# A decoder block on one core: the place at which the second half's normalised input is computed

## The chip, the cores and the metric

The kernel runs on one core of a Trainium2 chip. The metric is device time in microseconds (us), taken as the median over several runs. A profile is one further execution that the hardware profiler recorded; its own time is given beside its span.

## The reference

One layer of a decoder block for a sequence of 1024 tokens of width 1024. What matters here is the first part: a normalised and modulated input `h`, a wide projection of it, two branches with gates, and their merge.

```python
mod = silu(c) @ w_ada + b_ada
shift1, scale1, gate1, shift2, scale2, gate2 = split(mod, 6)
h = modulate(rms_norm(x, norm1_w), shift1, scale1)      # h * (1 + scale) + shift
q, k, v, r, a_lr, su, sv, g_a, g_b = split(h @ w_in)
...
o_gla = rms_norm(gla_chunked(q, k, v, log_a), gla_norm_w) * silu(r)
o_sgu = spatial_gating(gelu(su), gelu(sv), sgu_w, sgu_b, sgu_ln_w, sgu_ln_b)
merged = sigmoid(g_a) * o_gla + sigmoid(g_b) * o_sgu
x = x + gate1 * (merged @ w_out)
h2 = modulate(rms_norm(x, norm2_w), shift2, scale2)
x = x + gate2 * peer(h2, ...)                           # product-key experts, top 16 of 16384
return rms_norm(x, final_norm_w)
```

`h` of a token depends on `x` and `c` alone. So `h` of the later tokens can be computed at any time before their projection.

## The kernel before

The sequence is worked off in two halves of 512 tokens (`hf` = 0 and 1). A half goes through the weight groups in this order: G_V0, G_V1, G_QK0, G_QK1 (with the linear attention's heads between them), G_SV0, G_SV1, G_R0, G_R1, G_A0, G_A1, G_SU0, G_SU1, G_B0, G_B1, then the output projection, the second norm and the routing of the experts. The second half also carries the experts' work of the first.

A weight group is a matrix of 1024 x 512. `group` calls `stream`, which runs over eight slices `k` of 128 rows. A slice is loaded on SP's queue into `wt` (five buffers, line 1386), split into a high part `wh` by ScalarE (ACT, line 1390) and a low part `wl` by VectorE (DVE, line 1392), four buffers each, and multiplied by TensorE (PE) with the high and low parts of `h`, which lie in `hTh` and `hTl`: three products for each of four PSUM banks `mm`, so 12 matmuls a slice (lines 184 to 187, and 190 to 192 for the first and the last slice) and 96 a group. Weights are made up to three slices ahead. After the last slice the four banks are evicted by the group's own function:

- `ev_r` (G_R0, G_R1): ACT computes tanh into `sg`, DVE multiplies with the bank (line 1624) and then with `ot` (line 1626). The bank is free after DVE's first operation.
- `ev_a` (G_A0, G_A1): ACT computes tanh (line 1632), DVE multiplies `ot` (line 1634). The bank is free after ACT.
- `ev_su` (G_SU0, G_SU1): ACT computes gelu into `us` (line 1449). The bank is free after ACT.
- `ev_b` (G_B0, G_B1): ACT computes tanh, DVE takes two operations on `us` and `ot`. The bank is free after ACT.

After each of G_SU0 and G_SU1 comes `mix(c)`: 16 matmuls of 128 x 128 into the same four banks (`sps`, line 1651) and 16 DVE operations that take them out (line 1655).

Side work is written as Python generators in queues. Each slice of `stream` ends with `step()`, which pumps each queue: one `next` for `qa` and one for `qm`. In the first half `qa` holds, from the end of the first group on, four `ada_row` generators (each sums eight slices of `w_ada` and stores a row of the modulation, 11 pumps) and, behind them, `next_h(HALF)` (14 pumps). `qm` holds the norms of the branches, `out_norm` and `gate_norm`; it is emptied by `qm.drain()` ahead of each `mix`. `qa.drain()` stands at the end of a half.

`next_h` computes `h` for the second half and stores it in `hn_d` in device memory. Four pumps load two tiles `xb` each (SP, line 1198) and square them on ACT with a running sum (line 1199). One pump makes the row of reciprocal roots: a sum and a multiply on DVE, a power on POOL, `dg` on DVE, a product of `ones` and `dg` on PE (line 1188), a copy `rrow` on ACT (line 1189). Nine pumps run over eight tiles: load `xt` (SP, line 1209), scale it (DVE, line 1212), round to `hi` with the shift (ACT, line 1215), take the rest `lo` (DVE, line 1216), and store both to `hn_d` (ACT's queue, line 1218). A load of slice k is emitted one pump ahead of its use. `xb` and `xt` share two buffers, `hi` has two and `lo` one. Each load on SP is held behind the weight load that was made last before it (`tc.issue_after(last_wt[0])`).

The second half begins by loading `hn_d` into `hTh` and `hTl` (line 1402).

The program is written in this order, and the build then lays out each engine's instruction order from simulated times (`schedule_with_timeline_sim=True`); `issue_after` pins an instruction behind another on its engine. On the chip every engine runs its list in order, and waits for semaphores.

Of the kernel before, what the change touches and what calls it, by code (L numbers as in the profile page):

```python
# [21 lines left out]
HALF = 512  # L22
# [59 lines left out]
def block_kernel(ctx: ExitStack, tc: tile.TileContext, x, xT, cT, w_ada, b_ada, b_adaT, n1T, w_inp, w_alr,  # L82
# [95 lines left out]
    def mm3s(sets, k):  # L178
        if k in (0, KD - 1):
            for ps, lh, ll, rh, rl, feat in sets:  # L180
                mm3(ps, lh, ll, rh, rl, k == 0, k == KD - 1)
            return
        for ps, lh, ll, rh, rl, feat in sets:
            nc.tensor.matmul(ps, lh, rh, start=False, stop=False)  # L184
            nc.tensor.matmul(ps, *((lh, rl) if feat else (ll, rh)), start=False, stop=False)  # L185
        for ps, lh, ll, rh, rl, feat in sets:
            nc.tensor.matmul(ps, *((ll, rh) if feat else (lh, rl)), start=False, stop=False)  # L187
# [857 lines left out]
    qa, qr, qp, qdir, qm, qf = Queue(), Queue(), Queue(), Queue(), Queue(), Queue()  # L1045
# [10 lines left out]
    with ExitStack() as pa:  # L1056
# [105 lines left out]
        def ada_row(c, r):  # L1162
            for acc in ada_acc(c):
                yield
            for _ in range(2):
                yield
            row_ = t4("adarow")
            nc.scalar.dma_start(row_[0:1], b_ada[:, c * D:(c + 1) * D])
            for n in range(2):
                sl = slice(n * 512, (n + 1) * 512)  # L1170
                ps = auxt([1, 512])
                nc.tensor.matmul(ps, ones[:, 0:1], acc[:, sl], start=True, stop=True)
                nc.vector.tensor_tensor(row_[0:1, sl], row_[0:1, sl], ps, op=OP.add)
            if r == 1:
                nrow = t4("nrow")
                nc.scalar.dma_start(nrow[0:1], n2_w)
                nc.vector.scalar_tensor_tensor(row_[0:1], row_[0:1], 1.0, nrow[0:1], op0=OP.add, op1=OP.mult)
            nc.scalar.dma_start(rows_d[r:r + 1, :], row_[0:1])
            yield

        def rstd_row(ss, eng, rrow):
            rstd = sm_p.tile([P, BH], F32, name="rstd")
            rstd_of(rstd, ss, D, eng)
            dg = t2("dg")
            nc.vector.tensor_tensor(dg.rearrange("p (i q) -> p i q", q=P), ident.unsqueeze(1).to_broadcast([P, BH, P]),
                                    rstd.unsqueeze(2).to_broadcast([P, BH, P]), op=OP.mult)
            rps = auxt([P, HALF])
            nc.tensor.matmul(rps, ones, dg, start=True, stop=True)
            nc.scalar.activation(rrow, rps, AF.Identity)
            return rrow  # L1190

        def next_h(t0):
            ss = sm_p.tile([P, 2, BH], F32, name="ss")
            for i in range(BH):
                for n in range(2):
                    xb = gl.tile([P, HALF], F32, name="xb", tag="qs")
                    with tc.issue_after(last_wt[0]):
                        nc.sync.dma_start(xb, x[t0 + i * P:t0 + (i + 1) * P, n * HALF:(n + 1) * HALF])
                    nc.scalar.activation(xb, xb, AF.Square, accum_out=ss[:, n, i:i + 1])
                yield  # L1200
            nc.vector.tensor_tensor(ss[:, 0], ss[:, 0], ss[:, 1], op=OP.add)
            rrow = rstd_row(ss[:, 0], nc.vector, gl.tile([P, HALF], F32, name="rrow", tag="ktok", bufs=1))
            yield
            xts = []
            for k in range(KD + 1):
                if k < KD:
                    xts.append(gl.tile([P, HALF], F32, name="xt", tag="qs"))
                    with tc.issue_after(last_wt[0]):
                        nc.sync.dma_start(xts[k], xT[k * P:(k + 1) * P, t0:t0 + HALF])
                if k:  # L1210
                    j, xt = k - 1, xts[k - 1]
                    nc.vector.scalar_tensor_tensor(xt, xt, scol[:, j:j + 1], rrow, op0=OP.mult, op1=OP.mult)
                    hi = gl.tile([P, HALF], F32R, name="hi", tag="kk")
                    lo = gl.tile([P, HALF], F32R, name="lo", tag="kt", bufs=1)
                    nc.scalar.activation(hi, xt, AF.Identity, bias=mod[:, j:j + 1])
                    nc.vector.scalar_tensor_tensor(lo, xt, mod[:, j:j + 1], hi.bitcast(F32), op0=OP.add, op1=OP.subtract)
                    for n, t in enumerate((hi, lo)):
                        nc.scalar.dma_start(hn_d[:, n, j], t.bitcast(F32))
                yield
# [176 lines left out]
        for hf in range(NHALF):  # L1396
# [7 lines left out]
            def stream(srcs, body, evac, npsum=4, post=None, again=False):  # L1404
                pss = [mm.tile([P, 512], F32, name="mm", tag="mm") for _ in range(npsum)]
                turn = WS // len(srcs) if again else 0
                for n in range(KD):
                    weights_ahead(LOOK + 1)
                    ws = [made.pop(0) for _ in srcs]
                    body((n - turn) % KD, ws, pss, n)  # L1410
                    if post and n in post:
                        post[n]()
                    step()
                for i in range(npsum):
                    evac(i, pss[i])

            def group(src, evac, feat, post=None):
                def body(k, ws, pss, n):
                    wh, wl = ws[0]
                    cuts = [slice(i * P, (i + 1) * P) for i in range(4)]  # L1420
                    if feat:
                        mm3s([(pss[i], wh[:, cs], wl[:, cs], hTh[:, k], hTl[:, k], True) for i, cs in enumerate(cuts)], n)
                    else:
                        mm3s([(pss[i], hTh[:, k, cs], hTl[:, k, cs], wh, wl, False) for i, cs in enumerate(cuts)], n)

                stream([src], body, evac, post=post)
# [18 lines left out]
            def ev_su(c):  # L1445
                def f(i, ps):
                    if c == 0:
                        us[i] = t4("us")
                    nc.scalar.activation(us[i][:, c * 512:(c + 1) * 512], ps, AF.Gelu)
                return f  # L1450
# [18 lines left out]
            if hf == 0:  # L1469
                with tc.issue_after(hlast[0]):  # L1470
                    nc.scalar.dma_start(wst, wsT)
                for g in range(8):
                    nc.gpsimd.affine_select(out=wst[:, g], in_=wst[:, g], pattern=[[1, P]], compare_op=OP.is_ge, fill=0.0,
                                            base=0, channel_multiplier=-1)
                for c, r in ((2, 0), (4, 1), (3, 2), (5, 3)):
                    qa.add(ada_row(c, r))
                qa.add(next_h(HALF))

            alh = t2("alh", F32R)
            all_ = t2("all_", F32R)  # L1480
# [139 lines left out]
            def ev_r(c):  # L1620
                def f(i, ps):
                    sg = t2("sg")
                    nc.scalar.activation(sg, ps, AF.Tanh, scale=0.5)
                    nc.vector.scalar_tensor_tensor(sg, sg, 1.0, ps, op0=OP.add, op1=OP.mult)  # L1624
                    o = ot[i][:, c * 512:(c + 1) * 512]
                    nc.vector.tensor_tensor(o, o, sg, op=OP.mult)
                return f

            def ev_a(c):
                def f(i, ps):  # L1630
                    sg = t2("sg")
                    nc.scalar.activation(sg, ps, AF.Tanh, scale=0.5)
                    o = ot[i][:, c * 512:(c + 1) * 512]
                    nc.vector.scalar_tensor_tensor(o, sg, 1.0, o, op0=OP.add, op1=OP.mult)
                return f
# [44 lines left out]
            qm.add(gate_norm())  # L1680
            for gid, ev in ((G_R0, ev_r(0)), (G_R1, ev_r(1)), (G_A0, ev_a(0)), (G_A1, ev_a(1))):
                group(w_inp[gid], ev, False)
            for c in range(2):
                group(w_inp[G_SU0 + c], ev_su(c), False)
                qm.drain()
                mix(c)
# [228 lines left out]
```

## Time and profile before

| | |
|---|---|
| median of 3 runs | 1419.35 us (1417.38 to 1422.0) |
| profiled execution | 1417.0 us, span 1415.3 us |
| mean granted TensorE clock | 0.976 of full speed |
| PE busy | 1346.5 us, 95% of the span |
| DVE busy | 1076.7 us, 76% |
| ACT busy | 698.2 us, 49% |
| POOL busy | 274.3 us, 19% |
| DMA | 348.15 MB, mean 246 GB/s |

Times in the profile are us from the span's start. A row of a timeline has the start, the length, the engine, the line of the kernel, the operation, what it writes and reads, and in brackets how long the engine had been idle before it and what ended that. A row of a stretch has, for each engine, the busy time and the number of instructions, then the granted clock, the DMA engines' share and GB/s. A row of a source line has the least, middle and greatest duration in ns, and the first and last start.

In the first half G_R1 ends at 259.4, G_A0 at 284.5, G_A1 at 306.3, G_SU0 at 328.0 and G_SU1 at 353.4; the instructions of `next_h` lie between 213 and 288.

### The profile page before, as it was taken

To read this page: it belongs to the slowest core of one execution; us is meant where nothing else is said; L and a number is where in the kernel's file an instruction comes from. 1 tells how busy PE (TensorE), PEld (TensorE's weight loads), DVE (VectorE), ACT (ScalarE), POOL (GpSimd) and SP (SyncE) were. 2 spreads that over 40 slices of the span, in tenths; PEclk is the share of its full clock that TensorE was granted. 3 is DMA by queue.
4 is the path that set the end of the run, shared out by engine and by line. 5 is a ranking of instruction groups with operands and counts; after the bars stand their busy time and mean duration, and the time that the engine had idled before them with its cause. 6 is when DMAs were issued, how large, how long until landed. Compare 5 with 4: busy or idle time off the path is not lost.

```text
span 1415.3 us, 19579 instructions
## 1 busy us (share of the span) xinstructions
PE 1346.5 (95%) x5998; PEld 1037.7 (73%) x5998; DVE 1076.7 (76%) x3066; ACT 698.2 (49%) x1568; POOL 274.3 (19%) x271
## 2 busy tenths in 40 slices
PE   8999999999999899998999999999998999889996
PEld 6678777788888888777777788887777876444553
DVE  7785778543458578798879788878798877799885
ACT  4454335333245355474444566555555554555552
POOL 0000002000000021332452142211111123444421
PEclk9999999999999999999999999999999999989999
DMA  9753556642257469857787699986688568897984
GB/s 325 240 210 125 179 161 214 221 133 88 84 168 243 156 203 325 280 146 267 245 295 263 226 345 342 328 327 227 219 313 296 196 228 313 340 362 302 416 299 190
DMA packets 123492, 348.15 MB, mean 246 GB/s; under 512 B 15385, under 2 KB 24857, under 8 KB 111346
## 3 DMA queue, kind: packets, MB, share of 16 engines
q0 software_dynamic: 31488, 163.85, 31.5%
q1 hardware_dynamic: 72240, 133.44, 28.1%
q10 hardware_dynamic: 19650, 49.54, 9.7%
q8 instruction: 48, 0.79, 0.2%
q14 instruction: 66, 0.54, 0.1%
HBM read 318.35 MB, written 28.42 MB: 245 GB/s over the span
## 4 chain that ended last, share of the span: by engine, by line
PE 43%; DVE 8%; DMA 6%; ACT 4%; issue 3%; POOL 0%; ACTq 0%; DVEq 0%; POOLq 0%
PE mm L184 7%; PE mm L185 7%; PE mm L187 6%; PE acc L609 6%; PE mm L190 3%; PE mm L191 2%; PE mm L192 2%; PE aux L1805 2%; DMA uv<-in_tab_dram,dix 2%; DVE uv L583 1%; PE hps L581 1%; DMA uvd<-in_down_dram,dix 1%; PE hps L582 1%; PE acc L628 1%; PE acc L629 1%
## 5 line engine op out<-in xcount | busy, mean ns | idle before, releaser
L1390 ACT ACTIVATE wh<-wt 128x512 fp32r<-128x512 f32 x344 | 212.4, 628 | 269.2 <-PE mm L185 117.3
L1392 DVE TENSOR_TENSOR wl<-wt,wh 128x512 fp32r<-128x512 f32 x344 | 231.4, 684 | 116.8 <-ACT wh L1390 54.9
L184 PE MATMUL mm<-wh,hTh 128*128 128x512 f32 x648 | 256.8, 397 | 3.5 <-ACT wh L1390 3.5
L185 PE MATMUL mm<-wh,hTl 128*128 128x512 f32 x648 | 256.0, 395 | 0.0
L187 PE MATMUL mm<-wl,hTh 128*128 128x512 f32 x648 | 203.1, 397 | 0.7 <-DVE wl L1392 0.7
L184 PEld LDWEIGHTS mm<-wh,hTh 128*128 128x128 f32 x648 | 122.5, 189 | 32.6 <-ACT wh L1390 4.3
L185 PEld LDWEIGHTS mm<-wh,hTl 128*128 128x128 f32 x648 | 122.4, 189 | 26.3 <-issue 0.8
L187 PEld LDWEIGHTS mm<-wl,hTh 128*128 128x128 f32 x648 | 121.0, 189 | 27.3 <-issue 1.3
L528 POOL DMA_INDIRECT uv<-in_tab_dram,ix x74 | 77.0, 1041 | 263.9 <-ACT ix L560 137.2
L184 PE MATMUL mm<-hTh,wh 128*128 128x512 f32 x240 | 96.8, 403 | 0.1
L185 PE MATMUL mm<-hTl,wh 128*128 128x512 f32 x240 | 95.0, 396 | 0.0
L583 DVE SCALAR_TENSOR_TENSOR uv<-uv,hps 128x512 f32<-128x512 f32 x112 | 74.6, 680 | 21.7 <-DMA uv<-in_tab_dram,ix 12.9
L190 PE MATMUL mm<-wh,hTh 128*128 128x512 f32 x216 | 86.4, 408 | 2.7 <-DVE sg L1624 2.7
L192 PE MATMUL mm<-wh,hTl 128*128 128x512 f32 x216 | 85.5, 396 | 0.0
L191 PE MATMUL mm<-wl,hTh 128*128 128x512 f32 x216 | 85.3, 395 | 0.1
L190 PE MATMUL mm<-hTh,wh 128*128 128x256 f32 (+1 forms) x208 | 71.5, 346 | 6.0 <-DVE q L1528 5.0
L191 PE MATMUL mm<-hTl,wh 128*128 128x256 f32 (+1 forms) x208 | 70.1, 338 | 3.8 <-DVE hTl L176 3.8
L187 PE MATMUL mm<-hTh,wl 128*128 128x512 f32 x240 | 71.7, 397 | 0.7 <-DVE wl L1392 0.7
L192 PE MATMUL mm<-hTh,wl 128*128 128x256 f32 (+1 forms) x208 | 68.7, 337 | 0.0
L621 DVE SCALAR_TENSOR_TENSOR vl<-uv,r,vh 128x512 fp32r<-128x512 f32 x82 | 59.7, 745 | 9.5 <-ACT vh L620 4.1
L609 PE MATMUL acc<-uv,W 128*128 128x512 f32 x132 | 63.3, 602 | 1.4 <-ACT W L598 0.8
L755 POOL DMA_INDIRECT uvd<-in_down_dram,dix x32 | 33.7, 1054 | 157.1 <-DVE dix L1790 40.0
(957 smaller groups left out, 2889.1 us busy)
## 6 DMA issues: line engine op xcount, KB each, us to landing
wt<-in_w_inp_dram SPq DMA_DIRECT2D x224, 256.0 KB
wt<-in_w_qp_dram SPq DMA_DIRECT2D x72, 256.0 KB
wada<-in_w_ada_dram SPq DMA_DIRECT2D x32, 512.0 KB
wt<-in_w_outp_dram SPq DMA_DIRECT2D x56, 256.0 KB
wada<-in_w_ada_dram SPq DMA_DIRECT2D x32, 256.0 KB
s_d<-so ACTq DMA_DIRECT2D x28, 256.0 KB
xt<-in_xT_dram SPq DMA_DIRECT2D x16, 256.0 KB
xr<-in_x_dram ACTq DMA_DIRECT2D x8, 512.0 KB
```

The lines of the kernel that those rows point to most:

```text
L184: nc.tensor.matmul(ps, lh, rh, start=False, stop=False)
L185: nc.tensor.matmul(ps, *((lh, rl) if feat else (ll, rh)), start=False, stop=False)
L187: nc.tensor.matmul(ps, *((ll, rh) if feat else (lh, rl)), start=False, stop=False)
L190: nc.tensor.matmul(ps, lh, rh, start=first, stop=False)
L191: nc.tensor.matmul(ps, lh, rl, start=False, stop=False)
L192: return nc.tensor.matmul(ps, ll, rh, start=False, stop=last).ins
L528: nc.gpsimd.indirect_dma_start(out=dst[:], out_offset=None, in_=src, in_offset=off)
L583: nc.vector.scalar_tensor_tensor(uv[0][:, sl], uv[0][:, sl], 1.0, hps, op0=OP.mult, op1=OP.mult, accum_out=r[:, 2 + n:3 + n])
L609: ins = nc.tensor.matmul(acc[:, sl], W, v[:, sl], start=first, stop=last).ins
L621: nc.vector.scalar_tensor_tensor(vl, v, r[:, 5:6], vh.bitcast(F32), op0=OP.mult, op1=OP.subtract)
L1390: nc.scalar.activation(wh, wt, AF.Identity)
L1392: nc.vector.tensor_tensor(wl, wt, wh.bitcast(F32), op=OP.subtract)
```

## The change

The line that adds `next_h(HALF)` to the queue `qa` is taken from behind the four `ada_row` and put behind the group G_A1 of the first half, ahead of G_SU0. By then `qa` is empty. Everything that `next_h` issues is the same; only the steps in which it is pumped differ.

```diff
                 for c, r in ((2, 0), (4, 1), (3, 2), (5, 3)):
                     qa.add(ada_row(c, r))
-                qa.add(next_h(HALF))
...
             qm.add(gate_norm())
             for gid, ev in ((G_R0, ev_r(0)), (G_R1, ev_r(1)), (G_A0, ev_a(0)), (G_A1, ev_a(1))):
                 group(w_inp[gid], ev, False)
+            if hf == 0:
+                qa.add(next_h(HALF))
             for c in range(2):
                 group(w_inp[G_SU0 + c], ev_su(c), False)
                 qm.drain()
```

## The prediction, made before the changed kernel was run

> **What bounds the kernel now.** I read the page's first two parts, then the busy time by stretch, one stretch for each weight group around the change, then TensorE's timeline for gaps, and last the rows of the moved work and what waited for it.
>
> ```profile
> span 1415.3 us, 19579 instructions
> PE 1346.5 (95%) x5998; PEld 1037.7 (73%) x5998; DVE 1076.7 (76%) x3066; ACT 698.2 (49%) x1568; POOL 274.3 (19%) x271
> core 0: us, PE busy (x) PEld busy (x) DVE busy (x) ACT busy (x) POOL busy (x), PEclk, DMA share, GB/s
> 213.00:243.00 30.00, 30.00 (x127) 22.94 (x126) 26.16 (x43) 15.17 (x35) 7.22 (x5) 1.00 0.69 234
> 243.00:281.00 38.00, 35.54 (x154) 28.46 (x153) 22.36 (x34) 15.07 (x25) 0.00 (x0) 1.00 0.61 205
> 281.00:305.00 24.00, 24.00 (x107) 19.79 (x107) 11.37 (x18) 9.24 (x16) 0.00 (x0) 1.00 0.49 159
> 305.00:328.00 23.00, 23.00 (x103) 19.05 (x102) 8.17 (x12) 8.41 (x15) 0.00 (x0) 1.00 0.31 95
> ```
>
> TensorE (PE) is busy 95% of the span, and in the first half's merge stage nearly without a break: only the stretch 243:281 has idle time (35.54 of 38 us). So what a move of DVE, ACT and DMA work can win or lose here is the gaps that it takes from PE or gives to it. The timeline of PE shows them:
>
> ```profile
> 259.36 0.39 PE L192 MATMUL mm<-wh,hTl 128*128 128x512 f32 x1
> 260.59 0.50 PE L190 MATMUL mm<-wh,hTh 128*128 128x512 f32 x1 [0.85 <-DVE sg L1624]
> 262.54 0.39 PE L187 MATMUL mm<-wl,hTh 128*128 128x512 f32 x1
> 263.85 0.50 PE L190 MATMUL mm<-wh,hTh 128*128 128x512 f32 x1 [0.93 <-DVE sg L1624]
> 274.41 0.39 PE L185 MATMUL mm<-wh,hTl 128*128 128x512 f32 x1
> 275.49 1.20 PE L187 MATMUL mm<-wl,hTh 128*128 128x512 f32 x4 [0.69 <-DVE wl L1392]
> ...
> 284.46 0.39 PE L192 MATMUL mm<-wh,hTl 128*128 128x512 f32 x1
> 306.25 0.39 PE L192 MATMUL mm<-wh,hTl 128*128 128x512 f32 x1
> 328.01 0.39 PE L192 MATMUL mm<-wh,hTl 128*128 128x512 f32 x1
> 811.37 0.50 PE L190 MATMUL mm<-wh,hTh 128*128 128x512 f32 x1 [0.91 <-DVE sg L1624]
> ```
>
> The rows at 259.36, 284.46, 306.25 and 328.01 are the last matmuls of the groups G_R1, G_A0, G_A1 and G_SU0. Their distances are 25.10, 21.79 and 21.76 us. A group is 96 matmuls, so one is 0.227 us and a step (12 matmuls) 2.72 us, and G_A0 is 3.33 us too long. The three gaps account for it. Taken start to start, less one matmul, they are 260.59 - 259.36 - 0.23 = 1.00, 263.85 - 262.54 - 0.23 = 1.08 and 275.49 - 274.41 - 0.23 = 0.85, together 2.93. The other 0.4 is the slower first matmul behind each gap (0.50 against 0.39), so I count 0.13 more for each: 1.13, 1.21 and 0.98.
>
> **The change, part by part.** Nothing is added or removed; the generator next_h moves in the queue qa. Before, it stood behind four ada_row of 11 pumps each, so with one pump a step its first pump was the 45th after the first group: step 4 of G_R0. Now it is added behind G_A1 and its first pump is step 0 of G_SU0: 3 + 8 + 8 + 8 + 1 = 28 steps later, 28 x 2.72 = 76 us. Its 14 pumps then end at step 5 of G_SU1. What moves:
>
> ```profile
> L1198 SPq DMA_DIRECT2D xb<-in_x_dram x8: 327/354/532, 213.3 to 228.0; - x8
> L1199 ACT ACTIVATE xb<-xb x8: 615/632/632, 217.3 to 231.0; 128x512 f32<-128x512 f32 x8
> L1209 SPq DMA_DIRECT2D xt<-in_xT_dram x8: 328/328/681, 230.4 to 276.1; - x8
> L1212 DVE SCALAR_TENSOR_TENSOR xt<-xt,scol,rrow x8: 744/752/753, 243.6 to 280.4; 128x512 f32<-128x512 f32 x8
> L1215 ACT ACTIVATE hi<-xt,mod x8: 722/724/730, 244.4 to 281.2; 128x512 fp32r<-128x512 f32 x8
> L1216 DVE SCALAR_TENSOR_TENSOR lo<-xt,mod,hi x8: 745/748/752, 245.1 to 286.4; 128x512 fp32r<-128x512 f32 x8
> L1218 ACTq DMA_DIRECT2D hn_d<-lo x8: 326/361/362, 246.8 to 287.2; - x8
> ```
>
> That is 16 loads on SP, 16 stores on ACT's queue (eight hi beside the eight lo), 8 x 0.63 + 8 x 0.72 = 10.8 us of ACT, 8 x 0.75 + 8 x 0.75 = 12 us of DVE, a few small operations, one power on POOL and one product of ones and dg on PE. The product costs PE the same in either place: nothing. The power no longer stands behind gate_norm's on POOL (five in 213:243, none from 243 on): nothing, since rrow is not waited for by PE.
>
> The consumer of hn_d is the second half's first load:
>
> ```profile
> L1402 SPq DMA_DIRECT2D hTl<-hn_d x8: 319/356/819, 541.1 to 561.2; - x8
> ...
> 264.32 0.75 DVE L1216 SCALAR_TENSOR_TENSOR lo<-xt,mod,hi 128x512 fp32r<-128x512 f32 x1
> 265.09 0.33 SPq L1209 DMA_DIRECT2D xt<-in_xT_dram  x1
> 269.16 0.75 DVE L1212 SCALAR_TENSOR_TENSOR xt<-xt,scol,rrow 128x512 f32<-128x512 f32 x1 [0.49 <-DMA xt<-in_xT_dram]
> 269.95 0.73 ACT L1215 ACTIVATE hi<-xt,mod 128x512 fp32r<-128x512 f32 x1 [5.99 <-DVE xt L1212]
> 274.08 0.75 DVE L1212 SCALAR_TENSOR_TENSOR xt<-xt,scol,rrow 128x512 f32<-128x512 f32 x1 [3.51 <-DMA xt<-in_xT_dram]
> ```
>
> The last store was issued at 287.2 and will be near 287 + 76 + 3.5 = 367 (3.5 for the mix between the groups): still 170 us ahead of the load at 541. Costed at nothing; that cover would have to shrink by 170 us.
>
> What does cost is these waits. Two xt buffers make a chain: a load of xt goes out when lo has released the buffer (lo ends 265.07, load 265.09), lands some 4 us later, and then xt, hi, lo follow. DVE works in order and sat up to 3.51 us before an xt; ACT sat 5.99 us before a hi, and SP held the weight loads behind the xt load. That made G_A0's second gap (DVE was at an xt when G_R1's eviction sg had to be made) and the third (wl late behind the 3.51 us wait). Those two go: 1.21 + 0.98 = 2.2 us. The first gap (1.13) I leave: at the same boundary of the second half, where no next_h runs, the row at 811.37 shows the same wait of 0.91. So the removal is worth 2.2, between 2.2 and 3.3.
>
> The same chain now runs from about 320 (243.6 + 76) to 367, through G_SU0's end, mix(0), G_SU1, mix(1) and into G_B0. There the end of a group looks like this:
>
> ```profile
> 326.40 2.64 ACT L1449 ACTIVATE us<-mm 128x512 f32<-128x512 f32 x4 [0.95 <-PE mm L192]
> 328.24 3.73 PE L1651 MATMUL sps<-svg,wst 128*128 128x128 f32 x32
> 329.41 1.12 DVE L1655 SCALAR_TENSOR_TENSOR us<-sps,sgub,us 128x128 f32<-128x128 f32 x4 [2.94 <-PE sps L1651]
> 331.73 0.48 PE L190 MATMUL mm<-wh,hTh 128*128 128x512 f32 x1
> ```
>
> The first of the four gelu evictions ends about 326.40 + 0.66 = 327.1, and PE needs its bank at 328.24: 1.2 us to spare on ACT. The first us eviction ends at 330.5 and PE needs the bank at 331.73: 1.2 us on DVE. At mix(0) the first two xt are due, which were loaded long before; the waits begin with the third. At mix(1), near 353.6, the seventh and eighth are due (76 + 3.5 after their old times, the last at 280.4 + 79.5 = 360). So one boundary, on two engines, is exposed. Bounds: nothing, or ACT's 5.99 less 1.2, 4.8 us, and DVE's 3.5 less 1.2, 2.3 us, 7.1 together. I take 1.2, what the like collision cost at 263.85, the nearest row, and half of the 0.98 of a late wl: 38 us of this chain brought one such, and beside next_h DVE is loaded about as before ((22.36 - 12) in 38 us there, 8.17 in 23 here), so I give it an even chance. Together 1.7.
>
> Sum: -2.2 + 1.7 = -0.5 us on the profiled execution, which took 1417.0 us (1.7 around its span); that lies 2.35 under the median of the three runs, 1419.35. I put the difference on the median: 1418.9. Less than 0.3% (4.3 us) can hardly be told from no change here.
>
> A rule weighed: the xt waited for at 269.16 had been issued at 265.09, 4.1 us before, at 205 GB/s, and the first xb needed 4.0 (213.3 to 217.3) at 234, so I take the waits over unchanged; the new stretch has 95 and what next_h brings. [...]
>
> **Rivals.**
> (a) Slower: one stall at mix(1) that is long enough to lower PE's clock. What such a stall costs is seen later in this trace:
>
> ```profile
> 470.60 0.58 PE L191 MATMUL mm<-hTl,wh 128*128 128x256 f32 x1 [2.57 <-DVE hTl L176]
> 465.00:470.00 5.00, 2.07 (x17) 1.62 (x15) 4.96 (x27) 2.56 (x6) 0.00 (x0) 0.98 0.56 213
> 470.00:475.00 5.00, 4.40 (x20) 4.40 (x21) 1.84 (x3) 0.63 (x1) 0.00 (x0) 0.50 0.02 3
> 475.00:480.00 5.00, 5.00 (x38) 5.00 (x37) 1.79 (x3) 1.89 (x3) 0.00 (x0) 0.83 0.32 107
> ```
>
> PE was idle 2.9 us of 465:470, and the granted clock was 0.50 in the next five and 0.83 in the five after: 2.5 + 0.85 = 3.35 us lost beyond the stall. The price here: ACT's 4.8 + 3.35 - 2.2 = +6.0, 1425.3. It decides from a gelu held back by more than 1.2 + 2.9 = 4.1 us. For it: ACT has sat 5.99 us behind one xt. Against: that was one wait in eight. [...]
> (b) Faster: the waits miss mix(1), and the shifted order also removes the pit at 465 to 480 (3.35): -3.3 - 3.35 = -6.7, 1412.7. The build lays out each engine's order from simulated times, so later orders can shift. For it: only that; nothing links the pit with next_h, which is through 100 us before.
> (c) The change doesn't do what it says: the layout starts next_h as early as its inputs allow, and its old place comes back. For: its first load went out some 15 us ahead of its step (213.3, while step 4 of G_R0 ends near 228: G_R1's end at 259.36 less a group, the product and three steps). Against: each load is held behind the last weight load made before it, so 76 us can't be gained. It gives 1419.35.
>
> **How the numbers follow.** The forecast with (c), and all sizes between -4.3 and +4.3: 0.62 (forecast 0.57, c 0.05). (a), or the same through later orders that get worse: 0.21. (b): 0.17. The forecast's own range is 1415.1 to 1423.6. The range for 8 in 10 reaches to most of both others: 1413.5 to 1425.5.
>
> **What would show it.** In the changed profile the xt rows lie between about 318 and 362, G_A0 is about 22 to 23 us long (from the last matmul of G_R1 to its own), the gaps of 0.93 and 0.69 are gone, and PE has new gaps near mix(1) or G_B0's start, released by gelu, us or wl, of 1 to 3 us. Wrong would be: a gap at G_B0 or G_SU1 above 4 us with a clock under 1.00 behind it; no new gap at all; or a time that differs by more than 4 us with this stretch alike, so that the difference came from behind 380 us, where I expect every stretch alike.

## The result: slower by about half a per cent

The changed kernel took 1424.02 us in the median of 20 runs, the kernel before on the same chip 1417.46 in the median of 20. The ratio is 1.0053, 95% interval 1.0035 to 1.0071. The forecast's likeliest case was no change; what came is nearest to rival (a): stalls with a lowered clock behind one of them, but at the ends of three groups and not at one.

The profiled execution of the changed kernel took 1415.62 us, the shortest of its 20 runs, so spans can't be compared as they stand: TensorE had a lead of 4.67 us before the moved work begins, over the same instructions in the same order (G_R0's first matmul starts at 208.41 instead of 213.08). I therefore compare a stage of TensorE's work: from the products of line 1172, inside G_R0, to the first product of line 1806 (before: 1805), behind G_B1 and the output projection. Before, the first loads and squares of the moved work lie up to 11 us ahead of this mark, but they cost TensorE nothing there: at the products the lead is still 4.67 us (219.38 instead of 224.05). First the kernel before, its two marks and the stage in one row (us, busy time of PE, PEld, DVE, ACT, POOL with instructions, granted clock, DMA share, GB/s):

```profile
224.05 1.45 PE L1172 MATMUL aux<-adacc,ones 128*1 128x512 f32 x3
462.76 1.94 PE L1805 MATMUL aux<-keyst,qt 128*128 128x128 f32 x15 [0.21 <-ACT qt L1772]
224.05:462.76 238.71, 235.34 (x1127) 195.01 (x1126) 138.62 (x234) 94.41 (x163) 7.36 (x7) 1.00 0.50 164
```

The changed kernel's page, and the same stage with the stretches around the move:

```profile
span 1413.9 us, 19574 instructions
PE 1337.7 (95%) x5998; PEld 1029.8 (73%) x5998; DVE 1077.3 (76%) x3066; ACT 697.6 (49%) x1568; POOL 277.6 (20%) x271
219.38:463.91 244.53, 236.88 (x1127) 196.17 (x1126) 138.42 (x233) 96.21 (x171) 7.37 (x7) 0.99 0.50 165
243.00:281.00 38.00, 38.00 (x170) 31.45 (x169) 16.34 (x25) 12.06 (x21) 0.00 (x0) 1.00 0.34 110
281.00:305.00 24.00, 21.73 (x96) 17.60 (x95) 8.37 (x15) 12.23 (x28) 1.01 (x1) 1.00 0.51 165
328.30:333.30 5.00, 4.95 (x15) 3.93 (x16) 5.00 (x15) 0.72 (x1) 0.00 (x0) 0.66 0.61 212
333.30:338.30 5.00, 5.00 (x24) 4.14 (x23) 1.43 (x3) 0.65 (x1) 0.00 (x0) 1.00 0.47 154
```

The same 1127 matmuls take 244.53 us instead of 238.71, 5.8 more. The old place is clean now: in 243 to 281 PE is busy for 38.00 of 38 us, where it was busy for 35.54. The loss has moved behind 281. TensorE's timeline shows where:

```profile
297.30 0.39 PE L192 MATMUL mm<-wh,hTl 128*128 128x512 f32 x1
299.95 0.50 PE L190 MATMUL mm<-wh,hTh 128*128 128x512 f32 x1 [2.27 <-ACT sg L1631]
...
325.81 0.72 PE L1650 MATMUL sps<-svg,wst 128*128 128x128 f32 x5
328.35 0.50 PE L190 MATMUL mm<-wh,hTh 128*128 128x512 f32 x1 [1.81 <-DVE us L1654]
...
329.72 0.63 PE L185 MATMUL mm<-wh,hTl 128*128 128x512 f32 x1
330.15 0.63 PE L187 MATMUL mm<-wl,hTh 128*128 128x512 f32 x1
...
351.61 0.39 PE L192 MATMUL mm<-wh,hTl 128*128 128x512 f32 x1
354.67 3.81 PE L1650 MATMUL sps<-svg,wst 128*128 128x128 f32 x32 [2.67 <-ACT us L1449]
```

There are three stalls, one at each end of a group that the moved work now passes, where there were three smaller ones in G_A0:

- Start of G_SU0: 299.95 - 297.30 - 0.23 = 2.42, with the slower first matmul (0.13) 2.55 us. PE waits for ACT's tanh out of the bank.
- Start of G_SU1, behind mix(0): idle 1.81; as these rows overlap by 0.24 where nothing waits (before: 328.24 + 3.73 against 331.73), and with the 0.13, 2.2 us. PE waits for DVE's eviction of the mix. Behind it the clock is 0.66 for five us: matmuls are 0.43 apart (329.72, 330.15) instead of 0.23. That is 5 x 0.34 = 1.7 us more.
- mix(1): 354.67 - 351.61 - 0.23 = 2.83 us. PE waits for ACT's gelu.

Together 9.3 us. Against the 3.3 us by which G_A0 was too long, that makes +6.0; the stage has +5.8. What the engines were doing at these three places is in their timelines. ACT:

```profile
290.00 0.63 ACT L1199 ACTIVATE xb<-xb 128x512 f32<-128x512 f32 x1 [3.44 <-DMA xb<-in_x_dram]
...
298.69 0.63 ACT L1199 ACTIVATE xb<-xb 128x512 f32<-128x512 f32 x1 [0.46 <-DMA xb<-in_x_dram]
299.32 0.58 ACT L1631 ACTIVATE sg<-mm 128x512 f32<-128x512 f32 x1
...
353.55 0.33 ACTq L1218 DMA_DIRECT2D hn_d<-lo  x1
353.93 2.06 ACT L1449 ACTIVATE us<-mm 128x512 f32<-128x512 f32 x4 [3.11 <-DVE lo L1216]
```

The tanh at 299.32 could have run when the bank was done, before 298; it stands in ACT's list behind a square of `xb` that waited for its load until 298.69. The gelu at 353.93 stands behind the issue of `lo`'s store at 353.55, which waits for `lo`. And DVE:

```profile
325.84 0.75 DVE L1212 SCALAR_TENSOR_TENSOR xt<-xt,scol,rrow 128x512 f32<-128x512 f32 x1 [3.02 <-DMA xt<-in_xT_dram]
326.51 0.74 DVE L1216 SCALAR_TENSOR_TENSOR lo<-xt,mod,hi 128x512 fp32r<-128x512 f32 x1
327.17 1.12 DVE L1654 SCALAR_TENSOR_TENSOR us<-sps,sgub,us 128x128 f32<-128x128 f32 x4
...
352.77 0.75 DVE L1216 SCALAR_TENSOR_TENSOR lo<-xt,mod,hi 128x512 fp32r<-128x512 f32 x1 [3.04 <-DMA hn_d<-lo]
```

The eviction of the mix at 327.17 stands behind an `xt` that sat 3.02 us for its load, and its `lo`. The `lo` at 352.77 waited 3.04 us until the store of the `lo` before it had read the one buffer. So the stall at mix(1) is a chain: store of `lo` to device memory, `lo` on DVE, store on ACT's queue, gelu on ACT, mix on PE.

### The profile page after: what moved, and what is told of

Its sections match the earlier page's. It is cut to its first block, busy times and chain, and to the rows that moved or that the text cites. A ratio compares the mean times of both kernels' runs of the same rounds, so it can differ in the third digit from the quotient of the medians.

```text
span 1413.9 us, 19574 instructions
## 1 busy us (share of the span) xinstructions
PE 1337.7 (95%) x5998; PEld 1029.8 (73%) x5998; DVE 1077.3 (76%) x3066; ACT 697.6 (49%) x1568; POOL 277.6 (20%) x271
## 4 chain that ended last, share of the span: by engine, by line
PE 39%; DVE 10%; DMA 7%; issue 4%; ACT 4%; POOL 0%; another core or an unknown queue 0%; DVEq 0%; ACTq 0%; POOLq 0%
PE mm L184 6%; PE mm L185 6%; PE mm L187 6%; PE acc L609 5%; PE mm L190 2%; PE mm L191 2%; PE mm L192 2%; DMA uvd<-in_down_dram,dix 2%; DMA uv<-in_tab_dram,ix 2%; DVE uv L583 2%; PE aux L1806 2%; DMA uv<-in_tab_dram,dix 1%; PE hps L581 1%; PE hps L582 1%; DVE uv L537 1%
```

## The experiments

The theories, by the names that the expectations use. **Q**, the in-order theory: ACT and DVE work their lists in order, and an instruction of `next_h` that waits (for a landing, or for a buffer that a store still reads) holds up the eviction behind it, so the cost arises only at ends of groups. **E**: the loss lies elsewhere, in a later stage. **M**: the loads land later in the new place. **D**: the place itself decides; the later `next_h` comes, the slower. E needs no experiment of its own: outside the stretch from 213 to 354 us, from G_R0 to mix(1), each engine has the same order of instructions before and after, but for four places behind 900 us where neighbours on ACT or DVE are swapped; on POOL the order is the same throughout. Medians and ratios are against the kernel before, run on the same chip; "stage" is the time between the two marks, 238.7 before and 244.5 after. (The stretch of 170.9 us in the expectations of e0 to e3 is a part of it.)

**Again, both kernels.** e0 and e10 are the changed kernel unaltered, e8 and e9 the kernel before; the last three are single executions.

> The changed kernel once more, for a second profile. Theory Q (in-order queues blocked by next_h at the ends of groups): the three gaps of TensorE come back at the same places, at the start of G_SU0 behind sg, at the start of G_SU1 behind us, at mix(1) behind gelu, 1.5 to 3 us each, and the stretch from the first matmuls of G_R0 to those of G_B1 takes 175 to 179 us, against 170.9 in the profile of before. The whole is 0.3% to 0.7% slower than before. Theory E (elsewhere: the loss does not lie in this stretch, since the profiled execution of the changed kernel was not longer than that of before): the gaps change place or go, and the stretch is within 2 us of 171. Theory M (memory: the loads land later in the new place): loads of xt need clearly more than the 3.5 to 4.4 us of before.

> The kernel before, for a second profile. Open is why the kernels with five buffers, whose time from adacc to keyst is 236.8 and 236.9 us against 238.7 in the one profile of before, are not 0.15% faster than before. Theory Q: the gaps of before in G_A0 (1.0, 1.1 and 0.85 us start to start) differ between executions, and here they sum to less: the time from adacc to keyst lies at 236.5 to 238. Rival: the gaps are the same in each execution (238.5 to 239), and the five buffers cost 2 to 3 us somewhere else.

> The kernel before, for a third profile. As for the second: Theory Q 236.5 to 238 us from adacc to keyst, with gaps that differ from the other two profiles; rival 238.5 to 239.

> The changed kernel, for a third profile. Theory Q: gaps at the starts of G_SU0, G_SU1 and mix(1) again, 1 to 4 us each, with 244 to 248 us from adacc to keyst; and the times of the three executions differ by how long the waits were and whether the granted clock fell behind one.

Measured: e0 1424.49 against 1413.91, ratio 1.0074 [1.0045, 1.0102], stage 247.32, with stalls at the same three places; e10 1422.5, stage 247.71. The kernel before took 1414.45 and 1412.76 (and 1405.83 in a further execution beside them, so that single executions tell little), stage 238.47 and 238.64, each time with its three gaps in G_A0 (0.64, 1.02, 0.58 and 0.71, 0.45, 1.18 us of idle time). I had expected 236.5 to 238; the loss in G_A0 is there each time, and its sum hardly varies. The three stages of the changed kernel (244.5, 247.3, 247.7) lie 7.9 us above the three of before (238.7, 238.5, 238.6) in the mean, 0.56% of 1417, against 0.53% and 0.74% between the medians: the whole difference lies in the stage. In e10 rival (a) stands in plain view at mix(1): PE, its stretches, and DVE's wait for `lo`'s store:

```profile
359.59 5.25 PE L1650 MATMUL sps<-svg,wst 128*128 128x128 f32 x32 [4.97 <-ACT us L1449]
354.60:359.60 5.00, 0.03 (x2) 0.04 (x1) 1.35 (x2) 1.38 (x3) 0.00 (x0) 0.96 0.44 143
359.60:364.60 5.00, 5.00 (x33) 5.00 (x33) 2.85 (x10) 1.83 (x4) 0.00 (x0) 0.70 0.28 87
357.70 0.75 DVE L1216 SCALAR_TENSOR_TENSOR lo<-xt,mod,hi 128x512 fp32r<-128x512 f32 x1 [3.99 <-DMA hn_d<-lo]
```

PE stood still for 4.97 us, and the mix behind it took 5.25 us instead of 3.81, at a clock of 0.70.

**More buffers, at the changed place.** e1 gives the loads of `xb` and `xt` five buffers instead of two and issues those of `xb` one pump and those of `xt` two pumps earlier; e2 takes `lo` from a pool of five buffers that it shares with other tiles (`t2`), instead of from its single one; e3 does both. (Where the expectations of e11 and e12 give `lo` two buffers, it is this pool too.)

```diff
 # e1
+tag, bufs = (("qs", 2), ("qs", 2), ("adc", 3), ("adc", 3), ("adc", 3))[nring[0] % 5]
+t = gl.tile([P, HALF], F32, name=name, tag=tag, bufs=bufs)
...
-if k < KD:   # load xt[k]
+if k + 2 < KD:   # load xt[k + 2]
 # e2
-lo = gl.tile([P, HALF], F32R, name="lo", tag="kt", bufs=1)
+lo = t2("lo", F32R)
```

> Changed place, and the loads of xb and xt go through five buffers instead of two and are issued two pumps earlier; orders behind the stretch are the same as in the changed kernel. Theory Q: the gaps at G_SU0 (sg behind the squares) and G_SU1 (us behind an xt) go, the one at mix(1) stays, since lo still has one buffer: the stretch takes 169.5 to 172.5 us, the whole 0.1% to 0.4% faster than the changed kernel, within 0.2% of before. Theory E: no change, 0.5% slower than before. Theory M: loads land as late or later with more of them in flight, the waits of DVE before xt stay at 14 us in sum, and the time stays.

> Changed place, and lo is written to the pool b2 with five buffers instead of the single one; loads as in the changed kernel. Theory Q: only the gap at mix(1) goes (2.7 us, with its slow first matmuls 2.9), the other two stay: the stretch takes about 174 us, the whole 0.2% faster than the changed kernel and 0.3% slower than before. Theory E: 0.5% slower than before. Theory M: the same as Q for lo's store, no change for the rest.

> Changed place with both: five load buffers and five for lo. Theory Q: no gap of TensorE above 0.5 us from G_R0 to G_B1, the stretch takes 167 to 168.5 us (170.9 less the 3.3 of the gaps of before), the whole 0.15% to 0.35% faster than before and 0.6% faster than the changed kernel. Theory E: still 0.5% slower than before. Theory M: somewhere between.

The rows of PE that waited over 0.7 us in the stage, e1, then e2 with a row of ACT, then e3. (A row of 0.70 behind G_B1, near 430, released by `wh`, stands in every profile of this document, those of before too, and is left out here and below.)

```profile
302.75 0.50 PE L190 MATMUL mm<-wh,hTh 128*128 128x512 f32 x1 [1.06 <-ACT sg L1641]
356.08 5.44 PE L1660 MATMUL sps<-svg,wst 128*128 128x128 f32 x32 [4.00 <-ACT us L1459]
```

```profile
299.99 0.50 PE L190 MATMUL mm<-wh,hTh 128*128 128x512 f32 x1 [2.19 <-ACT sg L1631]
325.18 2.94 PE L1650 MATMUL sps<-svg,wst 128*128 128x128 f32 x24 [0.97 <-ACT us L1449]
341.70 0.50 PE L184 MATMUL mm<-wh,hTh 128*128 128x512 f32 x1 [2.38 <-ACT wh L1390]
340.41 0.72 ACT L1215 ACTIVATE hi<-xt,mod 128x512 fp32r<-128x512 f32 x1 [4.20 <-DMA hn_d<-hi]
```

```profile
303.13 0.50 PE L190 MATMUL mm<-wh,hTh 128*128 128x512 f32 x1 [1.14 <-ACT sg L1641]
```

e1: 1418.68, ratio 1.0039 [1.0021, 1.0058], stage 243.8. With loads ahead, the stall at G_SU1 goes and that at G_SU0 is less than half; at mix(1), where the wait is for `lo`'s store, it grows to 4.00. e2: 1419.92, 1.0042 [1.0016, 1.0068], stage 244.0. With the pool for `lo`, the stall at mix(1) goes, the one at G_SU0 stays at 2.19, and a late `wh` inside G_SU1 takes 2.38 in its stead. There ACT had waited 4.20 us before a `hi`, whose two buffers were still being stored: the chain's next link. Each half alone therefore wins little, and both miss their forecasts: the stage was to be longer than before by -1.4 to 1.6 us (e1) and about 3.1 (e2), and is by 5.1 and 5.3. Both together (e3): 1412.47, 0.9991 [0.9972, 1.0010], stage 236.8, 7.7 us under the changed kernel's profiled 244.5 and 1.9 under before; less was gained than I had expected (2.4 to 3.9 under before, no gap above 0.5, the whole 0.15% to 0.35% faster than before). The place is the same as in the changed kernel and so is the work; what is gone is most of the waiting in the queues: DVE waited 2.2 us before `xt` and `lo`, against 17.3 in the changed kernel. That is Q, and it is why D can't be the whole cause.

**Other places.** With the old buffers, e5 adds `next_h` ahead of G_A0, and e6 four steps earlier than the changed kernel (ahead of G_A1, behind four idle steps). With both longer rings, e7 stands two steps earlier than the change, e11 six steps later, and e12 at the old place.

```diff
             for gid, ev in (... (G_A0, ev_a(0)), (G_A1, ev_a(1))):
+                if hf == 0 and gid == G_A0: qa.add(next_h(HALF))                       # e5
+                if hf == 0 and gid == G_A1: qa.gens += [iter([None] * 4), next_h(HALF)] # e6; e7: 6
                 group(w_inp[gid], ev, False)
-            if hf == 0:
-                qa.add(next_h(HALF))    # e11: stays here, as qa.gens += [iter([None] * 6), next_h(HALF)]
```

> The two xt buffers and the one lo buffer as they were, next_h added ahead of G_A0: 16 steps before the changed place, 12 behind the old. Its waits now meet the ends of G_R1, G_A0 and perhaps G_A1, and no mix; orders behind the stretch are those of the changed kernel. Theory Q (an in-order wait costs where a group's eviction stands behind it): gaps at the starts of G_A0 (behind sg) and of G_A1 (behind sg), none at mix(0) or mix(1); between before and the changed kernel, 0.1% to 0.5% slower than before; the time from the first product of adacc in G_R0 to the first product with keyst is 239 to 244 us (238.7 before, 244.5 and 247.3 in the two profiles of the changed kernel). Rival D (distance: the later next_h comes, the slower, whatever stands beside it): the same 0.2% to 0.3%, but with gaps where no eviction waits.

> Buffers as they were, next_h four steps before the changed place (added ahead of G_A1 with four idle pumps), so that the squares fall into the middle of G_A1 and all four sg of its end stand in front of nothing of next_h. Theory Q: the gap at the start of G_SU0 (2.2 and 2.3 us in the changed kernel) goes, those at G_SU1 and mix(1) stay in some size: 0.1% to 0.3% faster than the changed kernel, the time from adacc to keyst 241 to 245 us. Rival D: within 0.1% of the changed kernel, with the gap at G_SU0 still there.

> Five load buffers and five for lo, next_h two steps before the changed place (ahead of G_A1 with six idle pumps), so that the squares end before G_A1's sg. Theory Q: the last gap of the kernel with both (1.14 us at the start of G_SU0) goes too: no gap above 0.5 us, the time from adacc to keyst about 235.5 us (236.8 with both, 238.7 before), the whole 0.15% to 0.3% faster than before. Rival D: as the kernel with both, 0.1% faster than before.

> The changed kernel with both longer rings (loads of xb and xt through five buffers, lo in two) and six idle steps put ahead of the part that computes the second half's input, so that all of it stands six steps later. With both rings at the unshifted place the only idle row of TensorE over 0.5 us was 1.14 us before group G_SU0, behind the squares of xb. In-order theory: the squares now fall inside G_SU0, where no product waits for ScalarE at once, so that row goes; no idle row over 0.5 us at G_SU0 or G_SU1, the stage from the first added product to the first key product 235.5 to 237 us, the whole 0.1 to 0.3% below the kernel before. Rival, that a gap only moves on to the next group end: an idle row of 1 to 3 us at G_SU1 or at the mix behind it, stage 238 to 240 us.

> The kernel before, with the part left at its old place beside the first half's gates, and both longer rings (five load buffers, lo in two). In-order theory: what cost time at either place is the wait of an engine's queue for a buffer or a landing at a group end; with both rings that wait is gone at the old place too, so the stage from the first added product to the first key product comes out at 236 to 237.5 us, within 1 us of the changed place with both rings (236.8), and the whole 0.05 to 0.2% below the kernel before. Rival, that the place itself matters: the stage stays near 238.5 us (the old place is worse by itself) or falls below 235.5 us (the changed place is worse by itself).

First the two of e5, whose queues have the old buffers; below it the one row of e7, of e11 and of e12:

```profile
262.03 0.79 PE L190 MATMUL mm<-wh,hTh 128*128 128x512 f32 x1 [2.87 <-DVE sg L1623]
315.25 0.79 PE L190 MATMUL mm<-wh,hTh 128*128 128x512 f32 x1 [6.31 <-ACT sg L1631]
```

```profile
323.92 3.81 PE L1660 MATMUL sps<-svg,wst 128*128 128x128 f32 x32 [1.30 <-ACT us L1459]
```

```profile
348.83 3.81 PE L1660 MATMUL sps<-svg,wst 128*128 128x128 f32 x32 [0.70 <-ACT us L1459]
```

```profile
261.00 0.50 PE L190 MATMUL mm<-wh,hTh 128*128 128x512 f32 x1 [2.09 <-DVE sg L1634]
```

- e5: 1424.14 against 1410.07, 1.0100 [1.0068, 1.0132], stage 249.4, the longest of all. No mix is touched, yet the evictions at the ends of G_R1 and G_A1 are held up, and PE stands still for 2.87 and 6.31 us. D falls: the earlier place is no better. Q's own forecast was missed in size (0.1% to 0.5%, stage 239 to 244) and in the second place, which was to be the end of G_A0; none of the gaps over 0.5 us lies there.
- e6: 1415.98, 1.0044 [1.0021, 1.0067], stage 240.8: with a shift of four steps G_SU0's stall goes, and smaller ones come at mix(0) (1.76), G_SU1 (0.76) and inside it (1.69, for a late `wl`); the one expected at mix(1) didn't come.
- e7: 1411.25, 1.0009 [0.9989, 1.0030], stage 236.9. I had expected no gap at all and 0.15% to 0.3% less than before; one of 1.30 stands at mix(0), and the whole is not clear of no change.
- e11: 1412.31 against 1413.32, 0.9987 [0.9967, 1.0006], stage 236.5. G_SU0's row went as expected, but one of 0.70 at mix(1) shows, a little above the 0.5 that I had set; the stage and the ratio are in the range forecast.
- e12: 1425.3, 1.0092 [1.0060, 1.0124], stage 239.3. A miss twice over. The stage was to fall to 237 and didn't, as the rival had it ("the old place is worse by itself"): a stall of 2.09 is left where G_A0 starts. Why, ACT and DVE of e12 show:

```profile
257.57 0.72 ACT L1225 ACTIVATE hi<-xt,mod 128x512 fp32r<-128x512 f32 x1 [0.73 <-DMA hn_d<-hi]
...
258.75 0.60 ACT L1633 ACTIVATE sg<-mm 128x512 f32<-128x512 f32 x1
```

```profile
258.33 0.75 DVE L1226 SCALAR_TENSOR_TENSOR lo<-xt,mod,hi 128x512 fp32r<-128x512 f32 x1 [0.70 <-ACT hi L1225]
259.00 0.68 DVE L1402 TENSOR_TENSOR wl<-wt,wh 128x512 fp32r<-128x512 f32 x1
259.60 0.74 DVE L1222 SCALAR_TENSOR_TENSOR xt<-xt,scol,rrow 128x512 f32<-128x512 f32 x1
260.26 1.87 DVE L1634 SCALAR_TENSOR_TENSOR sg<-sg,mm 128x512 f32<-128x512 f32 x3
```

The tanh is made at 259.35, but DVE has `lo`, `wl` and `xt` ahead of the multiply that frees the bank, 0.9 us more, part of it pushed back by `hi`, whose two buffers now wait for their stores. So at this end of a group, whose bank needs ACT and then DVE, work in the list added to the waits, and Q in its strict form, waits alone, was too narrow. How much of the 2.09 is work and how much the waits of `hi` (0.73 us in the row shown), no run separates. The second miss: the whole is 12 us over before, and the stage holds 0.7 of it. In this kernel the layout gave the second half other orders on all engines than before and after have, and most of the rest arises there: behind the stage its profile has 960.2 us, the three of before 951.0 to 953.1 (PE is busy for 97.07 us of 860 to 960 against 100.00 before, for one). So its total says nothing on the place, and which of those orders costs it is left open.

Over the other kernels of this section the total follows the stage: stage differences to before (238.6) of +8.7, +5.2, +5.4, -1.8, +10.8, +2.2, -1.7 and -2.1 us for e0, e1, e2, e3, e5, e6, e7 and e11 are 0.61, 0.37, 0.38, -0.13, 0.76, 0.16, -0.12 and -0.15%, each inside the interval of its measured ratio except e6, whose 0.16% lies just below its 0.21 to 0.67, and e7, just below its -0.11. All eight measured ratios lie above these figures, by 0.02 to 0.28%; what adds the 0.2 to 0.3% in e5, e6 and e7 is not shown.

## Why the prediction was wrong, point by point

- **The gain** was put at 2.2, with 3.3 as the bound; it is the bound. The first gap (1.13) went too: no matmul waits at G_R1's end in the changed kernel. The row at 811.37, which I took as proof that this end always costs 0.9, belongs to a second half whose ACT and DVE carry other work: there DVE's multiply at 810.63 stands behind an operation of the experts (line 588, 1.23 us) that had waited 1.45 us for its own load.
- **The cost: this is the step that failed.** "So one boundary, on two engines, is exposed", priced at 1.2 and 0.5 = 1.7 us. Three boundaries were exposed, and they cost 2.55, 2.2 and 2.83, with 1.7 of clock 9.3 us.
  - The squares of `xb` at G_A1's end were not priced at all, only counted as 0.63 us of ACT each. The quoted rows were enough to see it: squares from 217.3 to 231.0, moved by 76, lie at 293 to 307, and G_A1's end, without the gaps, at 303. They wait for their loads as `xt` does.
  - mix(0) was excused because "the first two xt are due, which were loaded long before". By the prediction's own shift the fourth was due there too: its row of before, below, moved by 76 us, is a wait from 328.6 to 332.1, and mix(0)'s evictions ran from 329.41 to 334.2. In the run the fourth `xt` stood at this mix, and waited 3.02 us.

```profile
256.13 0.75 DVE L1212 SCALAR_TENSOR_TENSOR xt<-xt,scol,rrow 128x512 f32<-128x512 f32 x1 [3.54 <-DMA xt<-in_xT_dram]
```

  - mix(1): the place was right, the mechanism wrong. I looked for a late `xt`. What held the gelu was `lo`'s single buffer and its store: I had named "lo one" as a fact and counted its stores as issues, and never asked how long a store keeps the buffer. Here that is 3.0 us of waiting, in e10 3.99. In e0 both stand in the chain: 2.87 us before the last `xt`, then 1.95 before the last `lo`.
- **The position.** Forecast: `xt` from 318 to 362. It came five to fourteen us earlier, mostly because the groups did: G_A1 ended at 297.30 instead of 306.25, of which 4.67 us is the lead of this execution and the rest what G_R1 and G_A0 no longer lose to the moved work. From G_A1's end the eight `xt` lie 15 to 50 us off, where 12 to 56 had been forecast:

```profile
L1198 SPq DMA_DIRECT2D xb<-in_x_dram x8: 328/328/1513, 285.4 to 299.4; - x8
L1209 SPq DMA_DIRECT2D xt<-in_xT_dram x8: 327/328/424, 305.4 to 343.9; - x8
L1212 DVE SCALAR_TENSOR_TENSOR xt<-xt,scol,rrow x8: 739/752/753, 312.7 to 347.7; 128x512 f32<-128x512 f32 x8
  DMA xt<-in_xT_dram: 14.3, 5
```

- **The waits, taken over unchanged.** The stretch wasn't lighter once `next_h` ran in it: 208 GB/s in 305 to 353, where its old place had 205 (243 to 281). So what a lighter load does was not shown. The waits were much the same: DVE waited 14.3 us for `xt` in all (last row above), against 12.2 before, and where it waited, a load was used 3.5 to 4.5 us after its issue in either place. Taking the waits over unchanged was right; the 95 GB/s were not the load to reckon with. M falls by the same numbers.
- **Rival (a)** had the right shape: a stall at mix(1) and a lowered clock, 1425.3 against the 1424.02 measured. Its price came from one stall of 4.8 with 3.35 of clock; in the profiled execution it was three of 2.2 to 2.8 with 1.7, in e10 mostly the one at mix(1). That the two times agree within 1.3 us is luck. Its condition, a gelu held back by more than 4.1 us, was too strict as well: the clock fell behind 1.81 us of idle time. I gave it 0.21 because "that was one wait in eight"; what counted is not how many waits there are but that each of the three ends of groups inside these 60 us met one. Rivals (b) and (c) fall: later orders are unchanged but for the four swaps, and the work is at its new place.
- **At no cost**, as forecast: the product of `ones` and `dg`, the power on POOL, and the use of `hn_d`, which came at 541.0, 187 us behind the last store's issue.

## What to carry to other kernels

Side work that waits (for a landing, for a buffer that a store still reads) cost less in the middle of a group here, where weights are made up to three slices ahead (a late `wl` or `wh` there: 0.6 to 1.2 us in the kernel before, 1.7 in e6, 2.4 in e2), and most at its end (1.81 to 2.67 us of idle time in the changed kernel's profile, 4.97 in e10, 6.31 in e5), where an eviction stands behind it in the same in-order list. So before moving it, mark every end of a group that its whole length passes, and for every operation in it, squares and stores as well, look up the wait in front of it. Free the waits first, all buffers of the chain together: one ring alone moved the stall to the next link here (4.00 us at mix(1) in e1, 2.38 inside G_SU1 in e2), both took most of it away (e3, stage 236.8 instead of 244.5), and then the place hardly mattered within eight steps (stages of 236.9, 236.8 and 236.5 in e7, e3 and e11). At the old place (e12) a stall of 2.09 was left.

## What the runs showed that I had not expected

- A stall of about 2 us was followed by a lowered clock of TensorE in some places and not in others. In the changed kernel's profile the five us behind the 1.81 at 328.35 had 0.66, while those behind 2.27 (299.95) and 2.67 (354.67) kept 1.00. In e0 the places are exchanged; its rows of stretches below are cut where the clock changes:

```profile
302.84 0.50 PE L190 MATMUL mm<-wh,hTh 128*128 128x512 f32 x1 [2.17 <-ACT sg L1631]
333.00 0.50 PE L190 MATMUL mm<-wh,hTh 128*128 128x512 f32 x1 [1.99 <-DVE us L1654]
300.58:303.99 3.41, 1.24 (x6) 0.97 (x6) 1.39 (x2) 2.05 (x5) 0.00 (x0) 1.00 0.62 187
303.99:307.41 3.42, 3.42 (x10) 2.64 (x9) 2.45 (x6) 3.00 (x8) 0.86 (x1) 0.50 0.31 120
331.30:334.71 3.41, 1.71 (x7) 1.43 (x8) 3.41 (x11) 0.70 (x1) 0.00 (x0) 1.00 0.37 127
334.71:338.13 3.42, 3.42 (x17) 2.83 (x16) 3.31 (x10) 0.73 (x1) 0.00 (x0) 1.00 0.54 201
```

  Of the eight stalls over 1.7 us in the three profiles of this one kernel, five were followed by 0.66 to 0.70 (1.81, 2.17, 2.46, 3.82 and 4.97 us of idle time) and three by 1.00 (1.99, 2.27 and 2.67). The length of the stall alone does not part the two: 1.81 was followed by a drop and 2.67 was not.

  The granted clock that these profiles recorded shows more. In the profile of before and in the changed kernel's, a drop inside the kernel is 3.41 us or 6.83 us at 0.50, so the shortest costs 1.7 us, and the drops begin whole multiples of 3.41 us apart (in the changed kernel's at 328.96, 472.32 and 642.98, for example). If the time is cut into pieces of 3.41 us at these points, the idle time inside one piece fits the outcome better than the length of the stall: the drops behind the eight stalls follow pieces with 1.81, 2.15, 2.17 and more us of idle time, while stalls of 1.99 and 2.27 us that a cut parted into 0.3 and 1.70, and 0.56 and 1.71, passed. Close to 1.8 it isn't sharp: one piece with 1.82 (352.85 to 356.26 in the changed kernel's profile) was followed by 1.00. Of the six stalls of 1.81 to 2.67 us, three cost themselves alone and three 1.7 us more.
- The part ahead of the stage, in which TensorE has the same order in the changed kernel and in the one before, differs between executions (its end stands at 221.1 to 224.1 in three profiles of before, at 219.4 to 222.6 in three of the changed kernel): by up to 4.7 us, where the change itself is 6.6. Marks around the stage, and not spans, made single profiles comparable.
